# Attention operands staged by halves of the tokens, the first halves one head earlier

## The chip, the cores and the metric

The kernel runs on one core of a Trainium2 chip. Its engines are TensorE (PE in the profile, and PEld for its weight loads), VectorE (DVE), ScalarE (ACT), GpSimd (POOL) and SyncE (SP), which here only issues DMAs. They work side by side and wait for each other by semaphores. The metric is the device time of one execution in microseconds (us); less is better.

## The reference

The program is a two-layer encoder over 1024 tokens of width 1024, in float32. Layer 0 mixes tokens with a gated block, layer 1 with attention; each layer ends with a gated feed-forward with a short convolution. The change touches the attention of layer 1 alone:

```python
def chunk_attention(h, k, v, w_q, rel_bias, w_o):
    """Each 64-frame chunk attends to its own chunk and the previous 8 chunks."""
    q = (h @ w_q).reshape(B, nc, CHUNK, N_HEADS, HEAD_DIM) * scale
    ...
    bias = rel_bias[:, rel_idx]                       # 16 heads, clipped relative position
    sc = jnp.einsum('bqhd,bkhd->bhqk', qb, kb) + bias
    p = jax.nn.softmax(sc, axis=-1)
    o = jnp.einsum('bhqk,bkhd->bqhd', p, vb)
    return o @ w_o
```

There are 16 heads of width 64. A block of 128 queries sees its own block of keys and the four before it, so a block of 128 keys is seen by five blocks of queries.

## The kernel before, in words

Nearly all matrix products are done in three passes of a narrower format: each operand is split into a high part and a low rest, and the products high by high, low by high and high by low are summed. The attention runs over heads in pairs. The projections q, k and v of pair p+1 are computed 128 rows (two heads) at a time while pair p is attended to: six products (q, k, v, each for two halves of 512 tokens) of 24 matmuls, handed out by a generator called `fill`.

One head is eight steps, one per block of 128 keys. Step i of head hd does `head.score(i)` (matmuls "st", lines 1122 and 1124), some matmuls of `fill`, pieces of the next head's maximum (`Max.block`, matmuls "mx", lines 1076 and 1083), `value` of the block two steps back (matmuls "po", lines 1152 to 1156), and the rest of its share of `fill`. An even head (the first of a pair) gets 12 matmuls of `fill` in each step, an odd one 6. So an even head takes some 34 us and an odd one some 24 us.

A score product needs q and k of one head in four tiles of 128 partitions: KM and QE (high parts, with constant rows and a row for the maximum in the other 64 partitions), KS and QS (high and low parts mixed). There are two sets of them, for even and for odd heads. The function `stage` fills a set: one POOL memset of the maximum's row of QE (line 973) and six DMAs from the projection's tiles thi and tlo (line 976), issued by SP. In the kernel before, the six DMAs of head hd+1 are issued in step 0 of head hd, each over all 1024 tokens (64 partitions of 4 KB, 256 KB). Head 0 alone is staged by halves already.

`Max` of head hd+1 loads the head's bias table (line 1066) in step 1 of head hd and takes the maximum over blocks: block 0 at the end of step 1, block 1 in the middle of step 2, block 2 at its end, and so on; the blocks 0 to 3 read only the first 512 tokens of QE and KM. DVE reduces each (junk, ma and mb, lines 1079 and 1085). After block 7 the maximum is transposed ("mr", line 1092), copied by ACT (line 1095), and written by SP as one row of 4 KB into QE (line 1096). The next head's first score needs that row.

PE's order is the order of the program; the other engines' and SP's orders are chosen by a scheduler that simulates the program, and once chosen each queue is worked off in order, so a DMA on SP that waits for its data holds up all DMAs behind it.

Of the kernel before, what the change touches and what calls it, by code (L numbers as in the profile page):

```python
# [18 lines left out]
P = 128  # L19
T = 1024  # L20
# [7 lines left out]
NH = 16  # L28
# [13 lines left out]
def f32(ap):  # L42
    return ap.bitcast(F32)
# [3 lines left out]
def trunk(ctx: ExitStack, tc: tile.TileContext, x, a_win, a_wv, a_wst, a_bs, a_wout, w_kv, w_q, w_o,  # L47
          f_win, f_wdown, bias, cst, consts, fgain, out):
    nc = tc.nc
    V, S, G = nc.vector, nc.scalar, nc.gpsimd  # L50
# [15 lines left out]
    def put_off(us, fn):  # L66
        pending.append((clock[0] + us, len(pending), fn))
        pending.sort(key=lambda e: e[0])
# [12 lines left out]
    def open_psum(n, bufs, small=4):  # L81

        psum["ctx"], psum["n"] = ExitStack(), n
        psum["a"] = psum["ctx"].enter_context(tc.tile_pool(name="pj", bufs=bufs, space=PSUM, reuse_waits="tile"))
        open_small(small)

    def open_small(bufs=4):
        psum["s"] = psum["ctx"].enter_context(tc.tile_pool(name="sm", bufs=bufs, space=PSUM, reuse_waits="tile"))
# [21 lines left out]
    def close_psum():  # L110
        psum["ctx"].close()
# [40 lines left out]
    def load_w(src, gain=None, pool=None, new=None, lo=None):  # L152
        raw = new_raw([P, KD, P])
        nc.sync.dma_start(raw, src)
        if gain is not None:
            with tc.issue_after(behind[G].ins):
                G.tensor_tensor(raw, raw, cc[:, gain:gain + KD].unsqueeze(2).broadcast_to([P, KD, P]), op=ALU.mult)
        if pool:
            w = tuple(pool.tile([P, T], F32R, tag=n, name=n).rearrange("p (k c) -> p k c", c=P) for n in ("whi", "wlo"))
            split(*w, raw, lo or V)  # L160
            return w
        ws = [(new or new_w)() for _ in range(2)]
        for i in range(2):
            split(*ws[i], raw.rearrange("p k c -> p (k c)")[:, halves[i]], lo if lo and i else V)
        return tuple(Halves(t) for t in zip(*ws))
# [24 lines left out]
    halves = [slice(0, H), slice(H, T)]  # L190
# [739 lines left out]
    QE, QS, KM, KS = ([b0.tile([P, T], F32R, name=f"{n}0")] for n in ("qe", "qs", "km", "ks"))  # L930
# [33 lines left out]
            S.copy(vT, ps)  # L964
            put_off(1.2, lambda: transpose_v(vT, t, hi, lo))

    def stage(hd, cs=slice(0, T)):

        p, c = divmod(hd, 2)
        own, oth = rows[c]  # L970
        q, k = parts[p, "q"], parts[p, "k"]
        if cs.start == 0:
            G.memset(f32(QE[c][own.stop % P:own.stop % P + 1, :]), 0.0)
        for dst, src in ((KM[c][own], k[0]), (QE[c][own], q[0]), (QS[c][own], q[0]), (QS[c][oth], q[1]),
                         (KS[c][own], k[1]), (KS[c][oth], k[0])):
            nc.sync.dma_start(f32(dst[:, cs]), f32(src[own, cs]))
# [14 lines left out]
    first("q", 0)  # L991
    first("k", 0)
    stage(0, halves[0])
    proj(psv[:, H:T], w2["v"], ys[1])
    for what in "qk":
        ps2[what, 1] = psS("qk")
        proj(ps2[what, 1], w2[what], ys[1])
        first(what, 1)
    stage(0, halves[1])
    wv_ctx.close()  # L1000
    catch_up()
# [14 lines left out]
    def load_o(k, t):  # L1016
        os_[t][k] = oh, ol = new_y()
        nc.sync.dma_start(f32(oh), osave[0, k, :, halves[t]])
        behind["o"] = nc.sync.dma_start(f32(ol), osave[1, k, :, halves[t]])

    hr = []
    with tc.tile_pool(name="b1", bufs=1, reuse_waits="tile") as b1, \
# [33 lines left out]
        def stage_v(p):  # L1056
            for dst, src in zip((VH[1], VL[1]), parts[p, "v"]):
                nc.sync.dma_start(f32(dst[:, :, 64:P]), f32(src))
# [142 lines left out]
        catch_up()  # L1201
        close_psum()
        open_psum(H, 2)
        mx = Max(0)
        for b in range(NB):
            put_off(4.0 + 0.8 * b, lambda b=b: mx.block(b))
# [7 lines left out]
        def output(todo):  # L1214

            for m, load, bank in todo:
                w = load()
                ps = bank("wo")
                yield from products(ps, w, os_[0], range(LAST), None)
                outs.append((m, w, ps))  # L1220
# [6 lines left out]
        for s in range(NH * NB):  # L1227
            hd, i = divmod(s, NB)
            p, c = divmod(hd, 2)
            if i == 0:  # L1230
                if c == 0:
                    pair = Pair(p)
                head = Head(hd, mx.bt, pair.done)
                mx = None
            n = (6 if c else 12) + (1 - 2 * c if i == 0 else 0)
            if p == LAST - 1 and c:
                n = 6 if i < 4 else 3
            if p == 0:
                n = (144 - early) * (s + 1) // 16 - (144 - early) * s // 16
            if p == LAST:  # L1240
                n = 5
                if c == 0 and i == LAG + 1:
                    for k in range(LAST):
                        load_o(k, 0)
                    todo = [(m, lambda m=m: ws.pop(m), psP if m < 2 else psS) for m in range(6)]
                    fill = chain(fill, output(todo[:3]))
                if s - LAST * 2 * NB in loads:
                    m = loads.index(s - LAST * 2 * NB)
                    with ExitStack() as after:
                        for ins in marks:  # L1250
                            after.enter_context(tc.issue_after(ins.ins))
                        ws[m] = load_w(w_o[m]) if m < 2 else load_w(w_o[m], new=new_y, lo=G)
            if s == NH * NB - 6:

                for i2 in range(4):
                    place = f32(bt.tile([P, T], F32R, tag=("thi", "tlo")[i2 % 2], name="hr"))
                    for j in range(2):
                        hr.append(place[:, halves[j]])
                        with tc.issue_after(behind["o"].ins):
                            nc.sync.dma_start(hr[-1], hsave[1][2 * i2 + j, :, halves[0]])  # L1260
            head.score(i)
            waiting.append((head, i))
            if i == 0 and hd + 1 < NH:
                stage(hd + 1)
            if i == (LAG if p < LAST else 5) and c == 0:
                stage_v(p)
            for _ in range(n // 2):
                next(fill, None)
            if hd + 1 < NH:
                if i == 1:  # L1270
                    mx = Max(hd + 1)
                for b in mid.get(i, ()):
                    mx.block(b)
                if i == 6:
                    put_off(0.5, mx.row)
            if len(waiting) > LAG:
                h0, b = waiting.pop(0)
                h0.value(b)
            for _ in range(n - n // 2):
                next(fill, None)  # L1280
            if mx:
                for b in end.get(i, ()):
                    mx.block(b)
# [176 lines left out]
```

## Time and profile before

| | us |
|---|---|
| median of 3 runs | 2173.44 (2172.83 to 2175.77) |
| the profiled execution's own time | 2177.01 |
| its span, first to last instruction | 2175.2 |
| PE busy in the span | 2137.3 |
| DVE, ACT, POOL busy | 1589.7, 1088.0, 680.0 |
| mean granted TensorE clock | 0.995 of full speed |

The attention with its interleaved projections lies between about 980 and 1445 us of the span. A busy PE means that a matmul was in flight; where PE is idle, the timeline names in brackets the idle time and what ended it. A wait for several semaphores is put down to the one that came last by the profile, so the name in the bracket has to be held against the other candidates.

### The profile page before, as it was taken

Reading aid. Unit: us, or ns where it says so; the run is one execution under the profiler, and the core shown is the slowest. Engines: PE = TensorE matmul, PEld = TensorE weight load, DVE = VectorE, ACT = ScalarE, POOL = GpSimd, SP = SyncE. Lnnn points to the kernel's source line nnn. Section 1 sums busy time; section 2 is a strip of 40 time slices with the busy share of each in tenths; the row PEclk is TensorE's granted clock in tenths of the full one; section 3 lists DMA queues with packets and bytes.
Section 4 is the critical chain, followed back from the end, with each engine's and each line's share of the span. In section 5 each row is a group of like instructions: output and inputs, shape, how many; then the busy total and the mean of one; then the engine's idle time right before and its main releaser. Section 6 shows DMA issues by size and latency. Waiting matters only on the chain.

```text
span 2175.2 us, 28369 instructions
## 1 busy us (share of the span) xinstructions
PE 2137.3 (98%) x9940; PEld 1781.5 (82%) x9940; DVE 1589.7 (73%) x2425; ACT 1088.0 (50%) x1913; POOL 680.0 (31%) x472
## 2 busy tenths in 40 slices
PE   8999999999999999999999999899999999999998
PEld 6888887888888888878888888787878888888887
DVE  4762879888888757675676666764988888885676
ACT  6544445544455544445555555552554455554443
POOL 0301324242334212144444443351343333331020
PEclk9999999999999999999999999999999999999999
DMA  5242233344445867635444455644144444568553
GB/s 208 78 133 90 83 111 121 141 177 148 169 166 198 285 208 237 227 96 123 121 109 109 114 126 127 192 159 173 59 170 155 165 168 136 179 237 305 195 192 136
DMA packets 151536, 344.06 MB, mean 158 GB/s; under 512 B 31840, under 2 KB 32224, under 8 KB 151392
## 3 DMA queue, kind: packets, MB, share of 16 engines
q1 hardware_dynamic: 148368, 336.78, 47.7%
q10 hardware_dynamic: 3024, 5.46, 0.7%
q8 instruction: 78, 1.28, 0.2%
q14 instruction: 66, 0.54, 0.1%
HBM read 225.20 MB, written 87.56 MB: 144 GB/s over the span
## 4 chain that ended last, share of the span: by engine, by line
PE 85%; DVE 9%; ACT 2%; DMA 2%; issue 2%; POOL 0%; SPq 0%; DVEq 0%; POOLq 0%; ACTq 0%
PE gate L869 9%; PE up L869 9%; PE up L362 6%; PE up L364 6%; PE up L367 6%; PE gate L362 5%; PE gate L364 5%; PE gate L367 4%; PE vps L473 4%; PE qkv L186 4%; PE qkv L182 3%; PE qkv L179 3%; DVE wlo L138 2%; PE st L1122 1%; PE po L1156 1%
## 5 line engine op out<-in xcount | busy, mean ns | idle before, releaser
L138 DVE TENSOR_TENSOR wlo<-raw,whi 128x512 fp32r<-128x512 f32 (+1 forms) x424 | 374.0, 892 | 233.6 <-ACT whi L137 233.5
L137 ACT CAST whi<-raw 128x512 fp32r<-128x512 f32 (+1 forms) x428 | 266.5, 628 | 335.7 <-PE gate L869 201.9
L362 PE MATMUL up<-yh,whi 128*128 128x512 f32 x688 | 268.2, 390 | 0.8 <-ACT gate L765 0.5
L364 PE MATMUL up<-yh,wlo 128*128 128x512 f32 x688 | 267.9, 389 | 0.0
L1136 POOL TENSOR_TENSOR pl<-p,ph 128x640 fp32r<-128x640 f32 (+4 forms) x128 | 160.2, 1258 | 170.9 <-ACT ph L1135 112.9
L726 POOL TENSOR_TENSOR h<-a 128x512 f32<-128x512 f32 x44 | 77.9, 1771 | 391.4 <-DVE a L718 391.4
L362 PE MATMUL gate<-th,whi 128*128 128x512 f32 x496 | 193.4, 390 | 3.0 <-ACT h L703 1.8
L364 PE MATMUL gate<-th,wlo 128*128 128x512 f32 x496 | 193.0, 389 | 0.0
L367 PE MATMUL up<-yl,whi 128*128 128x512 f32 x688 | 183.9, 389 | 0.0
L362 PEld LDWEIGHTS up<-yh,whi 128*128 128x128 f32 x688 | 129.1, 188 | 29.3 <-ACT gate L765 2.7
L138 DVE TENSOR_TENSOR yl<-raw,yh 128x512 fp32r<-128x512 f32 x180 | 145.2, 811 | 10.6 <-ACT yh L137 10.4
L367 PEld LDWEIGHTS up<-yl,whi 128*128 128x128 f32 x688 | 129.1, 188 | 26.9
L364 PEld LDWEIGHTS up<-yh,wlo 128*128 128x128 f32 x688 | 129.1, 188 | 26.6
L182 PE MATMUL qkv<-yh,wlo 128*128 128x512 f32 x336 | 134.7, 401 | 0.0
L179 PE MATMUL qkv<-yh,whi 128*128 128x512 f32 x336 | 132.9, 395 | 0.0
L367 PE MATMUL gate<-tl,whi 128*128 128x512 f32 x496 | 132.6, 389 | 0.0
L137 ACT CAST whi<-S 128x512 fp32r<-128x512 f32 x160 | 99.1, 619 | 64.8 <-PE up L367 58.1
L869 PE MATMUL up<-yl,whi 128*128 128x512 f32 (+1 forms) x312 | 120.6, 387 | 0.0
L869 PE MATMUL up<-yh,whi 128*128 128x512 f32 (+1 forms) x312 | 120.4, 386 | 0.0
L869 PE MATMUL gate<-yh,wlo 128*128 128x512 f32 (+1 forms) x312 | 120.4, 386 | 0.0
L869 PE MATMUL up<-yh,wlo 128*128 128x512 f32 (+1 forms) x312 | 120.3, 386 | 0.0
L869 PE MATMUL gate<-yh,whi 128*128 128x512 f32 (+1 forms) x312 | 120.2, 385 | 0.0
(268 smaller groups left out, 5260.4 us busy)
## 6 DMA issues: line engine op xcount, KB each, us to landing
raw<-in_f_win SPq DMA_DIRECT2D x88, 512.0 KB
gT<-h SPq DMA_DIRECT2D x88, 256.0 KB
h<-in_f_wdown SPq DMA_DIRECT2D x44, 512.0 KB
dS<-h SPq DMA_DIRECT2D x88, 256.0 KB
raw<-dS SPq DMA_DIRECT2D x40, 512.0 KB
raw<-gT SPq DMA_DIRECT2D x40, 512.0 KB
gB<-a SPq DMA_DIRECT2D x66, 256.0 KB
raw<-in_f_wdown SPq DMA_DIRECT2D x30, 512.0 KB
```

What stands on the lines that cost most here:

```text
L137: behind[S] = S.copy(hi, src)
L138: return eng.tensor_tensor(lo, src, f32(hi), op=ALU.subtract)
L179: nc.tensor.matmul(ps, wh[:, k, :], xs[k][0], start=k == 0, stop=False)
L182: nc.tensor.matmul(ps, wl[:, k, :], xs[k][0], start=False, stop=False)
L186: nc.tensor.matmul(ps, wh[:, k, :], xs[k][1], start=False, stop=k == last)
L362: nc.tensor.matmul(ps, wh[:, k, :], xs[k][0], start=first and k == 0, stop=False, skip_group_check=True)
L364: nc.tensor.matmul(ps, wl[:, k, :], xs[k][0], start=False, stop=False, skip_group_check=True)
L367: nc.tensor.matmul(ps, wh[:, k, :], xs[k][1], start=False, stop=k == 3, skip_group_check=True)
L473: nc.tensor.matmul(ps, a, b, start=k == i == 0, stop=k == KD - 1 and i == 2)
L726: G.tensor_tensor(B[n], x, B.get(y) if isinstance(y, str) else y, op=ALU.subtract)
L869: nc.tensor.matmul(ps[:, cs], w[:, ms], x[:, cs], start=q == i == 0 and p in (1, 6, 5, 4), stop=q == NP - 1 and i == 2, skip_group_check=True)
L1136: marks[2] = G.tensor_tensor(pl[:, :n], pf[:, :n], f32(ph[:, :n]), op=ALU.subtract)
```

## The change

`stage` now always takes a half of the tokens. The second half of head hd+1 is staged where all of it was (step 0 of head hd); the first half of head hd+2 is staged in step 6 of head hd, the seventh step, so a step or two before head hd+1 begins and a full head before that head's own `Max` of hd+2 reads it. The set being filled is then the one that head hd itself is using; by step 6 only its second 512 tokens are still read. The first half of head 1, which has no head -1, is staged before head 0. The memset of QE's row goes by halves too. Each head so has 12 DMAs of 128 KB (64 partitions of 2 KB) where it had 6 of 256 KB, and two memsets of 512 elements for one of 1024.

```diff
-    def stage(hd, cs=slice(0, T)):
+    def stage(hd, cs):
...
-        if cs.start == 0:
-            G.memset(f32(QE[c][own.stop % P:own.stop % P + 1, :]), 0.0)
+        G.memset(f32(QE[c][own.stop % P:own.stop % P + 1, cs]), 0.0)
         for dst, src in ((KM[c][own], k[0]), (QE[c][own], q[0]), (QS[c][own], q[0]), (QS[c][oth], q[1]),
                          (KS[c][own], k[1]), (KS[c][oth], k[0])):
             nc.sync.dma_start(f32(dst[:, cs]), f32(src[own, cs]))
...
         open_psum(H, 2)
+        stage(1, halves[0])
         mx = Max(0)
...
             if i == 0 and hd + 1 < NH:
-                stage(hd + 1)
+                stage(hd + 1, halves[1])
+            if i == 6 and hd + 2 < NH:
+                stage(hd + 2, halves[0])
```

PE's order does not change at all. SP's changes as follows. The first place is the passage from head 2 (even) to head 3 (odd), as it repeats at every such passage: names ending in 8153 to 8156 are the even heads' set, 8463 to 8466 the odd heads'. Before:

```order
L154 DMA raw<-in_w_kv 128x1024
L1096 DMA qe_8463<-mr 1x8x128
L976 DMA qe_8153<-thi 64x1024
L976 DMA qs_8154<-thi 64x1024
L976 DMA qs_8154<-tlo 64x1024
L1066 DMA bias<-in_bias 128x512
L976 DMA km_8155<-thi 64x1024
L976 DMA ks_8156<-thi 64x1024
```

The same place on SP now (8464 is the odd heads' QE here):

```order
L975 DMA qe_8153<-thi 64x512
L975 DMA qs_8154<-thi 64x512
L975 DMA qs_8154<-tlo 64x512
L154 DMA raw<-in_w_kv 128x1024
L975 DMA km_8155<-thi 64x512
L975 DMA ks_8156<-thi 64x512
L975 DMA ks_8156<-tlo 64x512
L1095 DMA qe_8464<-mr 1x8x128
L975 DMA qe_8153<-thi 64x512
L975 DMA qs_8154<-thi 64x512
L975 DMA qs_8154<-tlo 64x512
L1065 DMA bias<-in_bias 128x512
```

Six half transfers now stand ahead of the row of the maximum, and six half transfers, not whole ones, behind it and around the bias.

The second place is SP at the passage from head 0 to head 1, where head 2 is staged. Before:

```order
L1096 DMA qe_8463<-mr 1x8x128
L976 DMA qe_8153<-thi 64x1024
L976 DMA qs_8154<-thi 64x1024
L976 DMA km_8155<-thi 64x1024
L976 DMA qs_8154<-tlo 64x1024
L976 DMA ks_8156<-tlo 64x1024
L976 DMA ks_8156<-thi 64x1024
L1066 DMA bias<-in_bias 128x512
```

Now:

```order
L1095 DMA qe_8464<-mr 1x8x128
L975 DMA qe_8153<-thi 64x512
L975 DMA qs_8154<-thi 64x512
L975 DMA km_8155<-thi 64x512
L975 DMA qs_8154<-tlo 64x512
L975 DMA ks_8156<-tlo 64x512
L975 DMA ks_8156<-thi 64x512
L1065 DMA bias<-in_bias 128x512
```

The bias stands behind half as many bytes; the other six halves stand ahead of the row of the maximum.

The third place is DVE at the start of head 14, where it works on the last projection's leftovers, on head 13's output and on head 15's maximum at once. Before:

```order
L1186 RECIPROCAL den<-den 128x128
L1128 TENSOR_TENSOR p<-st,bias 128x256
L1186 RECIPROCAL den<-den 128x128 x2
L1079 ISA junk,mb<-mx,bias 128x128
L1079 ISA mb 128x1
L138 TENSOR_TENSOR wlo<-raw,whi 128x512
```

Now:

```order
L1185 RECIPROCAL den<-den 128x128
L1078 ISA junk,mb<-mx,bias 128x128
L1078 ISA mb 128x1
L1127 TENSOR_TENSOR p<-st,bias 128x256
L1185 RECIPROCAL den<-den 128x128 x2
L138 TENSOR_TENSOR wlo<-raw,whi 128x512
```

The reduction of block 0 moved ahead of a score's bias addition and two reciprocals. In step 1 of head 1 the same reduction moved ahead of one bias addition. Apart from two pairs of neighbours on ACT and the memsets on POOL, nothing else moved.

## Rows read from the trace of the kernel before

**Rows 1.** The page: the span, and busy time by engine.
```profile
span 2175.2 us, 28369 instructions
...
PE 2137.3 (98%) x9940; PEld 1781.5 (82%) x9940; DVE 1589.7 (73%) x2425; ACT 1088.0 (50%) x1913; POOL 680.0 (31%) x472
```
**Rows 2.** PE's waits, 940 to 1445 us: total us, times, longest.
```profile
PE mx L1076 <- DVE o L1174: 5.8, 5, 1.5
PE st L1122 <- DVE mb L1079: 3.1, 2, 2.6
PE st L1122 <- DVE ma L1085: 2.2, 1, 2.2
PE st L1122 <- DMA qe<-mr: 1.8, 1, 1.8
...
PE mx L1076 <- DMA km<-thi: 1.1, 2, 0.9
```
**Rows 3.** Timeline of PE: start, us, instruction [idle before, what ended it].
```profile
1028.42 0.40 PE L1122 MATMUL st<-qe,km 128*128 128x256 f32 x1 [2.59 <-DVE mb L1079]
...
1084.09 0.30 PE L1076 MATMUL mx<-km,qe 128*128 128x128 f32 x1 [0.91 <-DMA km<-thi]
...
1142.56 0.30 PE L1076 MATMUL mx<-km,qe 128*128 128x128 f32 x1 [1.46 <-DVE o L1174]
...
1375.18 0.30 PE L1076 MATMUL mx<-km,qe 128*128 128x128 f32 x1 [0.62 <-DVE o L1174]
```
**Rows 4.** Timeline of SP (start, us to issue), odd heads 3, 5 and 13.
```profile
1074.21 0.72 SPq L1096 DMA_DIRECT2D qe<-mr  x1
...
1079.19 0.79 SPq L976 DMA_DIRECT2D km<-thi  x1
...
1137.12 0.81 SPq L976 DMA_DIRECT2D km<-thi  x1
...
1370.34 0.79 SPq L976 DMA_DIRECT2D km<-thi  x1
```
**Rows 5.** Timeline of DVE, the copy named in rows 2, heads 5 and 13.
```profile
1141.01 0.68 DVE L1174 COPY o<-po 64x512 f32<-64x512 f32 x1 [1.18 <-ACT den L1173]
...
1374.47 0.68 DVE L1174 COPY o<-po 64x512 f32<-64x512 f32 x1 [1.45 <-ACT den L1173]
```
**Rows 6.** Timeline of SP and of DVE in head 1.
```profile
1016.27 0.54 SPq L976 DMA_DIRECT2D qe<-thi  x1
...
1022.29 1.24 SPq L1066 DMA_DIRECT2D bias<-in_bias  x1
...
1028.07 0.29 DVE L1079 CUSTOM_DVE_ANT_0 junk<-mx,bias 128x128 f32<-128x128 f32 x1 [4.77 <-DMA bias<-in_bias]
```
**Rows 7.** Windows: us, busy us of five engines, granted clock, DMA share, GB/s.
```profile
1028.00:1032.00 4.00, 3.58 (x11) 3.11 (x12) 2.47 (x11) 1.62 (x3) 2.56 (x2) 0.58 0.02 7
...
1136.00:1140.00 4.00, 4.00 (x25) 3.51 (x23) 3.83 (x10) 3.62 (x8) 0.10 (x1) 1.00 1.00 229
...
956.00:962.00 6.00, 6.00 (x24) 4.51 (x23) 5.10 (x7) 2.86 (x5) 6.00 (x5) 0.92 0.61 143
```
**Rows 8.** Timeline, end of head 2: k's rest on DVE, head 3's first score.
```profile
1072.98 0.63 DVE L961 TENSOR_TENSOR tlo<-qkv,thi 128x512 fp32r<-128x512 f32 x1
...
1078.61 0.28 PE L1122 MATMUL st<-qe,km 128*128 128x256 f32 x1
```
**Rows 9.** Timeline, from head 1 to head 2: the maximum's row, the first score.
```profile
1042.04 0.70 SPq L1096 DMA_DIRECT2D qe<-mr  x1
...
1044.34 0.28 PE L1122 MATMUL st<-qe,km 128*128 128x256 f32 x1
```
**Rows 10.** Timeline of PE in head 14.
```profile
1406.19 0.58 PE L1122 MATMUL st<-qe,km 128*128 128x256 f32 x1 [2.22 <-DVE ma L1085]
...
1407.54 0.69 PE L1122 MATMUL st<-qe,km 128*128 128x384 f32 x1 [0.55 <-DVE mb L1079]
```
**Rows 11.** The memsets of line 973 on POOL: count, ns min/median/max, first and last.
```profile
L973 POOL MEMSET qe<- x16: 942/947/950, 940.1 to 1390.0; 1x1024 f32 x16
```

## The prediction

> **What bounds the kernel now.** I read the page first, then PE's waits in the attention, then the timelines around each wait. The page says that PE is busy for 2137.3 of 2175.2 us [rows 1]: whatever this change gives has to come out of the 38 us in which PE stands, and in the attention that is a handful of places. PE's waits from 940 to 1445 us name them [rows 2]. Two lines are about the matmul "mx": 5.8 us put down to a DVE copy (5 times) and 1.1 us put down to the DMA of km (twice). Three are about "st", and the longest of those is 2.6 us. The timeline shows where they stand. The mx waits are one per pair, always at the same matmul: block 0 of the next head's maximum, at the end of step 1 of an odd head [rows 3] (1084.09, 1142.56 and 1375.18 are three of six; the seventh of the two lines is 0.2 us in head 1). The 2.6 us are one wait in head 1, at 1028.42.
>
> What does the mx matmul really wait for? The label says a copy of o on DVE, and a label is only the last releaser that the profile knows. Between that copy's end and mx lie 0.87 us in head 5 (1141.69 to 1142.56) and 0.03 us in head 13 (1375.15 to 1375.18) [rows 3, 5]: no fixed distance, so it releases nothing. From the issue of km's DMA to mx it is 4.90, 5.44 and 4.84 us in heads 3, 5 and 13 [rows 3, 4]: a transfer's time, with the load of the queue in its scatter. So all six wait for km, whose transfer of all 1024 tokens can be issued only once the second half of k has been evacuated at the head's start. That is the first thing that the change removes.
>
> The wait in head 1 is of another kind. DVE's reduction of block 0 stood 4.77 us for the bias table [rows 6], the maximum's PSUM tiles stayed occupied, and PE ran out of them 2.59 us before 1028.42 [rows 3]. The bias was issued at 1022.29, behind six whole transfers whose first was issued at 1016.27 [rows 6], and landed about 1028.0.
>
> **Term 1: six waits for km, and 0.2 us in head 1.** Block 0 reads only the first 512 tokens. These are now issued a head ahead (in an odd head's queue the halves ahead of mr are the other set's), so when PE comes to mx they have been in place for some ten us. The second half is needed by block 4, two steps later, and is issued at the same time as before with half the bytes. In the instruction list of the changed kernel block 0 and block 4 each wait for DMAs of their own, so the parts are kept apart. Removed: 5.8 + 1.1 = 6.9 us [rows 2]. What is late next is DVE's reduction of block 0, which had been waiting for mx itself; PE has four tiles before it needs that one back.
>
> **Term 2: the bias in head 1.** From 1016.27 to 1028.0 the queue moved six times 0.262 MB and the bias' 0.262 MB, 1.83 MB in 11.8 us, or 156 GB/s. Now it is six times 0.131 and 0.262, 1.05 MB; at 156 GB/s that is 6.7 us, so the bias lands at about 1023.0. DVE began to wait at 1028.07 - 4.77 = 1023.3 [rows 6], PE at 1025.8. Removed: 2.59 us. After the wait the clock fell: in 1028 to 1032 the granted clock is 0.58 [rows 7], between 1.2 and 2.4 GHz, so 0.84 of 4 us ran at the lower level and half of it, 1.7 us, was lost. The short waits for km have no such window behind them. Removed with the wait: 1.7 us.
>
> **Term 3: DVE's order in head 14.** The reduction of block 0 moves ahead of an addition and two reciprocals, so the tile that 1407.54 waited for comes back earlier (0.55 us, [rows 10]), while the wait of 2.22 us before it, for a later reduction, stays. Between nothing and 2.77 us I take the nearer row, 0.5 us. The 1.8 us for the row of the maximum [rows 2] stay too, since there the row is late for want of matmuls to cover it.
>
> **What is added.** 90 DMA issues on SP (15 heads, 12 for 6) at 0.5 to 0.8 us each. SP stands idle for much of each head, so the issues cost nothing by themselves; what counts is what stands behind them. Ahead of mr there are now six halves. In an odd head their data has long been there and they are free once score 3 is issued, some ten us before mr. In an even head three of them wait for the first half of k: the last for its rest, which DVE ends at 1072.98 + 0.63 = 1073.61 [rows 8]. Its issue takes about 0.6 us, so mr, issued at 1074.21 before [rows 4], goes out 0.1 to 0.6 us later, and its 4 KB run behind 0.13 to 0.4 MB. At the 229 GB/s of a full DMA window [rows 7] that is 0.6 to 1.7 us. Head 3's first score starts 4.40 us after mr's issue [rows 4, 8], and where an odd head ends 2.30 us are enough with no wait of PE [rows 9]. The slack is 2.1 us, the delay 0.7 to 2.3: hidden but for perhaps 0.2 us in some heads. I charge 0.3 us in all. The bounds: no cost, and 1.3 us a passage if all six were ahead (0.79 MB at 229 GB/s are 3.4 us, less 2.1).
>
> Do halves cost more per byte? The trace has six: those of head 0 from 956.5 on. In 956 to 962 the DMA engines moved 143 GB/s at a share of 0.61 [rows 7], 234 GB/s for a full share, against 229 for whole ones. So no.
>
> The Trainium skill, "DMA: Bandwidth & Descriptors", section "Anatomy of one DMA", speaks against the change: it puts a fixed 2 us on each DMA, whatever its size (measured there on GpSimd's path). If those added up, six halves in a row would be late by nearly as much as six wholes, and term 2 would be gone. The window of head 0's halves does not bear it out: they overlap.
>
> The memsets become two of 512 elements for one of 1024 at 0.95 us [rows 11]: the same elements, between 0 and 0.95 us more per head on POOL. The first waits in POOL's queue for score 3 just ahead of the subtraction that needs score 3 itself, so it holds up nothing that could have run. No cost.
>
> **Sum**: 6.9 + 2.6 + 1.7 + 0.5 - 0.3 = 11.4 us. The profiled execution took 2177.0 us, so 2165.6; it was 3.6 us above the median of the three runs, and against that median of 2173.4 the forecast is 2162 us, 0.5% faster.
>
> **Rivals.**
> *The label is right (12%).* If mx does wait for DVE's copy, the 5.8 us of the five waits stay [rows 2], and the gain is 5.6: 2168 us. For it: five of seven waits carry that name. Against it: the uneven distances above.
>
> *Halves take as long as wholes (12%).* Then the bias lands as late as before and term 2 stays: gain 11.4 - 4.3 = 7.1, 2166 us. For it: descriptors of half the size, twice as many. Against it: the window at 956.
>
> *Both, or the km wait gives way to another one (8%).* A gain of 0 to 4 us, no change that can be told: 2171 us. PE has no other wait in those steps now, but nothing shows how near the next one is.
>
> *Slower: the row of the maximum lands behind the halves (7%).* Place: mr at every passage. If all six halves are still in flight when it is issued, it lands 3.4 us later. At the seven passages into an odd head 2.1 of these are hidden, 1.3 are not; at the seven into an even head, whose 2.30 us leave next to nothing [rows 9], 3.4 cost in full: 7 x 4.7 = 33 us, 2195 us. It decides from a mean of 1.1 us lost per passage on, where the 14 passages take up the 11.7 us gained and 4.3 more. For it: three of the halves in an even head are issued within two us of mr. Against it: in odd heads, where the slack is small, they are ten us ahead.
> The Trainium skill ("DMA: Bandwidth & Descriptors", "Queues, rings and completion order") says that what one engine issues goes through one ring on each DMA engine and is worked off in ring order. By that rule the row cannot pass the halves; no row here shows the two next to each other.
>
> **Numbers.** The forecast has 61%, with a range of its own from 2157 to 2166. The range for eight in ten takes in the two rivals beside it and the bounds of terms 2 and 3: 2157 to 2170. About 0.2%, 4.3 us, is what a measurement of this kernel can tell from no change. Faster: 61 + 12 + 12 = 85%; the same 8%; slower 7%.
>
> **What would show it.** In the new profile PE's waits for mx at the end of step 1 of odd heads are gone (right) or stand there with the same 0.6 to 1.5 us (the label was right). The bias of head 1's reduction lands before 1024 us and the granted clock near 1030 is 1.00. The issue of mr to the next first score is still 4.4 us in even and 2.3 us in odd heads, without a wait. New waits of PE for "qe<-mr" would make the prediction wrong on the slower side; new waits for DVE's reductions in place of km would make it wrong on the side of no change.

## The result, and the profile after

The changed kernel takes 2161.1 us (median of 4 runs, 2159.2 to 2164.8) beside 2174.6 us for the kernel before (4 runs, 2172.8 to 2176.7). The ratio is 0.9935, with a 95% interval from 0.9922 to 0.9947. The forecast was 2162 us, 0.5% faster; it is 0.65% faster by this ratio, 0.62% by the medians. The profiled execution took 2162.3 us.

Line numbers from `stage` on are one lower than before (mx 1075, st 1121, mr 1091, the scaling on POOL still 157). The page of the new profile, its span and busy times, answers to [rows 1]:

```profile
span 2160.5 us, 28590 instructions
...
PE 2131.3 (99%) x9940; PEld 1777.6 (82%) x9940; DVE 1592.7 (74%) x2425; ACT 1087.9 (50%) x1913; POOL 680.6 (31%) x488
```

PE's idle time went from 37.9 to 29.2 us, and its busy time fell by 6.0 us with the same 9940 matmuls, for the most part because less of it lies at the lower clock (below). PE's waits in the attention, the largest of 935 to 1445 us (total, times, longest), answer to [rows 2]:

```profile
PE st L1121 <- DVE mb L1078: 3.1, 1, 3.1
...
PE mr L1091 <- DVE mb L1086: 1.4, 1, 1.4
...
PE st L1121 <- DMA qe<-mr: 1.2, 1, 1.2
```

No line with mx and km or with the copy of o is left, and the 3.1 us are another wait than before: it stands in head 14, not in head 1. From 994.7 to 1380 us, so from head 0 to the end of head 13, no wait of PE is left. The timeline of PE at the end of step 1 of head 3, where [rows 3] had 0.91 us, now reads:

```profile
1078.62 0.40 PE L182 MATMUL qkv<-yh,wlo 128*128 128x512 f32 x1
1078.86 0.23 PE L1075 MATMUL mx<-km,qe 128*128 128x128 f32 x1
1078.91 0.33 PE L1121 MATMUL st<-qe,km 128*128 128x256 f32 x1
```

The mx matmul starts without a bracket, 0.24 us behind its predecessor's start, and takes 0.23 us where after a wait it took 0.30. In head 1, the bias on SP, DVE's first reduction and the window that [rows 6, 7] showed:

```profile
1021.03 0.59 SPq L1065 DMA_DIRECT2D bias<-in_bias  x1
```
```profile
1024.19 0.29 DVE L1078 CUSTOM_DVE_ANT_0 junk<-mx,bias 128x128 f32<-128x128 f32 x1 [0.41 <-DMA bias<-in_bias]
```
```profile
1028.00:1032.00 4.00, 4.00 (x27) 3.64 (x26) 2.54 (x11) 2.54 (x6) 2.95 (x3) 1.00 0.78 182
```

DVE waits 0.41 us for the bias where it waited 4.77, PE not at all, and the granted clock is 1.00 (of 2.4 GHz) where it was 0.58. The bias is issued in 0.59 us, where it took 1.24 behind six whole transfers.

Where the time went, head by head: I take the start of the first "st" matmul behind each "mr" matmul as a mark (for head 0 its first score, from then on the score of the eighth step of the head in front), and the gain of a head is its distance between two marks before less the same distance in another kernel (us; "start" is the mark of head 0, before less that kernel).

| kernel | start | head 1 | 3 | 5 | 7 | 9 | 11 |
|---|---|---|---|---|---|---|---|
| the change | -1.11 | 5.00 | 1.17 | 1.70 | 1.71 | 1.15 | 1.63 |
| split_only | -0.41 | 5.00 | 1.17 | 1.70 | 1.70 | 1.16 | 1.63 |
| bias_first | 1.34 | 2.56 | 0.37 | 0.59 | 0.71 | -0.04 | 1.41 |
| km_split | -0.05 | 0.91 | -0.11 | 0.49 | 0.60 | -0.17 | 1.63 |
| late_bias_first | -8.85 | 5.00 | 1.16 | 1.71 | 1.70 | 1.15 | 1.64 |
| km_split_pool | 1.52 | 1.10 | 1.17 | 1.70 | 1.71 | 1.15 | 1.63 |
| km_pool_bias | 2.36 | 5.00 | 1.16 | 1.70 | 1.71 | 1.15 | 1.63 |

For the change, heads 13 and 14 add 2.7 us together, and the even heads 4 to 12 lie within 0.01 us of before. The column "start" also holds the 980 us ahead of the attention, where PE does the same work in all these kernels and yet the executions lay apart: at the matmul that starts at 975 us in the kernel before, km_pool_bias was 2.25 us ahead of it, km_split_pool 1.42, bias_first 1.21, split_only 0.57, the change 0.31, and km_split and late_bias_first 0.17 and 0.31 behind. Without that, the start itself costs the change 1.4 us, split_only 1.0 and late_bias_first 8.5; the other four gain 0.1. The table's other kernels are the experiments, which follow.

### The profile page after: what moved, and what is told of

Its sections match the earlier page's. It is cut to its first block, busy times and chain, and to the rows that moved or that the text cites. A ratio compares the mean times of both kernels' runs of the same rounds, so it can differ in the third digit from the quotient of the medians.

```text
span 2160.5 us, 28590 instructions
## 1 busy us (share of the span) xinstructions
PE 2131.3 (99%) x9940; PEld 1777.6 (82%) x9940; DVE 1592.7 (74%) x2425; ACT 1087.9 (50%) x1913; POOL 680.6 (31%) x488
## 4 chain that ended last, share of the span: by engine, by line
PE 85%; DVE 9%; DMA 2%; ACT 2%; issue 1%; POOL 0%; DVEq 0%; SPq 0%; POOLq 0%; ACTq 0%
PE gate L869 9%; PE up L869 9%; PE up L362 6%; PE up L364 6%; PE up L367 6%; PE gate L362 5%; PE gate L364 5%; PE gate L367 5%; PE vps L473 4%; PE qkv L182 4%; PE qkv L179 4%; PE qkv L186 3%; DVE wlo L138 2%; PE po L1155 1%; PE po L1153 1%
```

## The experiments

**split_only: the place of the calls.**
```diff
-        stage(1, halves[0])
...
             if i == 0 and hd + 1 < NH:
-                stage(hd + 1, halves[1])
-            if i == 6 and hd + 2 < NH:
-                stage(hd + 2, halves[0])
+                for hs in halves:
+                    stage(hd + 1, hs)
```


> The changed kernel, but both halves of a head's transfers are called for in step 0 of the head in front; the calls in the seventh step, and the one ahead of head 0's maxima, are gone. What stays of the change is the split alone. Theory A (the split makes the whole gain; the place of the call decides nothing, since every transfer goes as soon as its source is written and its buffer free): the same time as the changed kernel, 2161 us within 2, ratio to the kernel before 0.993 to 0.994, and the same waits of PE. Theory B (the early call carries the gain): the first halves are issued later, waits for km of 0.5 to 1.5 us come back in the odd heads, and the time lies at 2166 to 2172 us.

Measured: 2164.5 us, ratio 0.9945 (0.9928 to 0.9962), and the gain of the heads 1 to 13 is the change's. The instruction lists of the two kernels are the same on all engines, so theory A holds, though the time lies 1.5 us above its range: the seventh step decides nothing, and what differs between the two is what one list does from execution to execution. In these two traces that is 0.4 us at the start and 0.7 us in the wait for the row of the maximum at head 14 (1.16 us in the change, 1.90 here); the medians lie 3.4 us apart, the ratios 0.0010. The scheduler issues a transfer as soon as its source is written and its buffer free, and a half is ready earlier than a whole.

**bias_first: the bias ahead of the wholes.**
```diff
             if i == 0 and hd + 1 < NH:
+                mx = Max(hd + 1)
                 stage(hd + 1)
...
-                if i == 1:
-                    mx = Max(hd + 1)
```


> The kernel before with one edit: the bias of the next head's maxima is called for ahead of the six whole transfers in step 0, so that SP issues it ahead of them. Theory A (the terms are separate: in head 1 the bias came late because six whole transfers stood in front of it, in the odd heads km came late because its own transfer is long): the 2.59 us wait in head 1 and the stretch at clock 0.58 go, 4.3 to 5.0 us; the waits for km in the odd heads stay, each 0 to 0.6 us longer since one more transfer is ahead of km. Time 2167 to 2172 us, ratio 0.9965 to 0.9990. Theory B (both waits come from the traffic of the whole transfers, and only halves take them away): the bias still lands late in head 1, and the time stays at 2173 to 2175 us.

Measured: 2168.6 us, ratio 0.9962 (0.9947 to 0.9976). The time is theory A's, the reason is neither's: the km waits went in all odd heads from 3 on but head 7 (0.74 us there), and head 1 gained half of what it should. SP's timeline of this kernel at the passage to head 3, to be held against [rows 4]:

```profile
1071.72 0.53 SPq L976 DMA_DIRECT2D qe<-thi  x1
1072.35 0.53 SPq L1066 DMA_DIRECT2D bias<-in_bias  x1
...
1075.58 0.46 SPq L976 DMA_DIRECT2D km<-thi  x1
```

From the first transfer's issue to km's are 3.86 us in both kernels, and the same four transfers stand ahead of km. But with the bias second, 189 GB/s were moved in the 4 us from the first issue, before 145; km then was there for an mx that ran 7.7 us after that issue, where before it was not at 7.8 us. Why the order of the four changes the rate is left open. PE waited elsewhere instead, here in head 1:

```profile
1031.43 0.39 PE L1156 MATMUL po<-pl,vh 128*128 128x256 f32 x1 [1.67 <-POOL pl L1136]
```

**km_split: one transfer of the six by halves.**
```diff
+        for part in (halves if cs == slice(0, T) else (cs,)):
+            nc.sync.dma_start(f32(KM[c][own, part]), f32(k[0][own, part]))
-        for dst, src in ((KM[c][own], k[0]), (QE[c][own], q[0]), ...
+        for dst, src in ((QE[c][own], q[0]), ...
```


> The kernel before with one edit: of a head's six transfers only km's is split by halves, the other five stay whole. Theory A (the first block of maxima waits for the length of km's one transfer, and half of it is enough): the six waits for km at the odd heads go, 6.9 us by PE's idle and up to 8.2 us by the starts of the heads; the bias in head 1, behind seven transfers now, is as late as before, so that its 2.59 us wait and its slow clock stay. Time 2166 to 2169 us, ratio 0.9960 to 0.9975. Theory B (the wait named km was the traffic of all six, or DVE's copies that feed the transfers): waits of 1 us or more stay at the odd heads, 2172 to 2175 us.

Measured: 2167.2 us, ratio 0.9957 (0.9943 to 0.9972). PE waits for km at no odd head any more, as theory A has it. In head 5, where the label put the wait down to DVE's copy of o, mx now starts before that copy does, so the copy cannot be what it waits for. PE and then DVE, to be held against [rows 3, 5]:

```profile
1140.12 0.23 PE L1078 MATMUL mx<-km,qe 128*128 128x128 f32 x1
```
```profile
1140.19 0.68 DVE L1176 COPY o<-po 64x512 f32<-64x512 f32 x1 [1.17 <-ACT den L1175]
```

But heads 3 to 9 give back nearly all of it at once. POOL's timeline at head 3, and then PE's:

```profile
1083.29 1.58 POOL L1138 TENSOR_TENSOR pl<-p,ph 128x640 fp32r<-128x640 f32 x1 [0.82 <-ACT ph L1137]
1088.35 1.90 POOL L157 TENSOR_TENSOR raw<-raw,cc 128x1024 f32<-128x1024 f32 x1 [3.48 <-DMA raw<-in_w_q]
1090.21 3.06 POOL L1138 TENSOR_TENSOR pl<-p,ph 128x640 fp32r<-128x640 f32 x2
```
```profile
1091.81 0.39 PE L1158 MATMUL po<-pl,vh 128*128 128x256 f32 x1 [1.03 <-POOL pl L1138]
```

The scaling of the next pair's q weights (L157) stands in POOL's queue ahead of the third pl and waits 3.48 us for its own transfer, and PE then waits for pl. The same row was there before, and the wait for km had covered it:

```profile
1088.88 1.90 POOL L157 TENSOR_TENSOR raw<-raw,cc 128x1024 f32<-128x1024 f32 x1 [3.11 <-DMA raw<-in_w_q]
```

SP issues that transfer last, and this is where the change differs (km_split first, then the change):

```profile
1080.38 0.69 SPq L978 DMA_DIRECT2D ks<-tlo  x1
1081.16 2.17 SPq L154 DMA_DIRECT2D raw<-in_w_q  x1
```
```profile
1076.97 0.46 SPq L975 DMA_DIRECT2D ks<-tlo  x1
1077.53 0.54 SPq L154 DMA_DIRECT2D raw<-in_w_q  x1
```
```profile
1081.90 1.90 POOL L157 TENSOR_TENSOR raw<-raw,cc 128x1024 f32<-128x1024 f32 x1 [0.27 <-DMA raw<-in_w_q]
```

With halves the issue takes 0.54 us, not 2.17, and POOL (last fence) waits 0.27 us: it starts on the weights 11.0 us behind head 3's mark, 14.2 in km_split and 13.8 before. Heads 11 and 13 scale no q weights any more, and there km_split has the whole gain: 1.63 us in head 11.

**late_bias_first: halves, held behind the row of the maximum.**
```diff
+                behind["mr"] = nc.sync.dma_start(f32(QE[self.c][row:row + 1, :]), f32(mr))
...
-        stage(1, halves[0])
...
             if i == 0 and hd + 1 < NH:
+                mx = Max(hd + 1)
+                with tc.issue_after(behind["mr"].ins):
+                    stage(hd + 1, halves[0])
                 stage(hd + 1, halves[1])
-            if i == 6 and hd + 2 < NH:
-                stage(hd + 2, halves[0])
```


> The changed kernel with the early part undone by force: the halves are called for in step 0, the first halves are held until SP has issued the row of the maximum, and the bias is called for ahead of them. Order on SP at a passage: mr, km's first half, bias, the other first halves, the second halves. Theory A (short transfers and a bias in front of them are enough, being early is not needed): no km wait, no bias wait, the time of the changed kernel within 3 us, 2158 to 2164. Theory B (the first halves must be under way ahead of the row of the maximum): waits of 1 to 1.5 us at the odd heads come back, some of the even heads wait too, and the time lies at 2167 us or above.

Measured: 2168.8 us, ratio 0.9968 (0.9957 to 0.9978). The total is theory B's, the heads are theory A's: from head 1 on each gains what it does in the change (head 6 lies 0.1 us under it). The loss is one wait of PE ahead of head 0's first score, with the clock at 0.50 from 1000.2 to 1006.8 behind it, and ACT's row says for whom:

```profile
1001.34 0.80 PE L179 MATMUL qkv<-yh,whi 128*128 128x512 f32 x1 [5.51 <-DVE tlo L958]
```
```profile
999.97 1.08 ACT L957 ACTIVATE thi<-qkv 128x512 fp32r<-128x512 f32 x2 [3.42 <-DMA qs<-thi]
```

The held halves of head 1 are still to be read from the tiles that the next projection writes. So early transfers are not needed for their own readers, with the bias in front as here; at the start they free their source. POOL has the scaling behind the third pl here, by the scheduler's own choice, and although the weights are issued only at 1088.46, behind twelve halves, PE does not wait for pl.

**km_split_pool: that instruction on POOL moved one place.** To km_split is added:
```diff
-            with tc.issue_after(behind[G].ins):
+            with tc.issue_after((behind.get("pl", behind[G]) if gain == C_BG else behind[G]).ins):
...
             head.score(i)
+            if c and i == 2 and p < LAST:
+                behind["pl"] = marks[2]
```


> The kernel before with km's transfer alone split by halves, as in the run of that edit, and one instruction moved besides: on POOL the scaling of the next pair's q weights (raw by cc) is held behind the third score's subtraction (pl) of an odd head, where it stood behind the second. Theory A (once km is early, PE's next wait in the odd heads, 1.03, 0.94, 0.83 and 1.06 us for pl in heads 3, 5, 7 and 9, is the weights' transfer: it lands late behind the whole transfers and the scaling that waits for it holds up pl in POOL's queue): these four waits go, 3.9 to 4.8 us, and the time lies at 2162 to 2164 us, ratio 0.9935 to 0.9950; head 1 still waits for its bias. Theory B (pl is late for another reason, POOL's own work or the memset of 1024 elements): the waits stay, 2166 to 2168 us.

Measured: 2165.8 us, ratio 0.9950 (0.9937 to 0.9962), a little above theory A's time. The four waits for pl are gone and heads 3 to 9 gain exactly what they do in the change. POOL at head 3 now reads, and the scaling's transfer is as late as ever (2.02 us to issue, at 1079.06):

```profile
1081.43 3.24 POOL L1138 TENSOR_TENSOR pl<-p,ph 128x640 fp32r<-128x640 f32 x2 [0.82 <-ACT ph L1137]
1086.13 1.90 POOL L157 TENSOR_TENSOR raw<-raw,cc 128x1024 f32<-128x1024 f32 x1 [1.46 <-DVE ma L1087]
```

**km_pool_bias: and the bias first.** To this is added the edit of bias_first.

> The kernel of the run above (km alone split, the scaling on POOL one place later) with the bias of the next head called for ahead of the other transfers as well. Theory A (three things make up the change's gain: km early, the bias not behind six whole transfers, the weights' scaling not in front of pl): head 1 gains 4.1 us more, by its 2.1 us wait and the slow clock behind it, and the time is that of the changed kernel or a little under, 2157 to 2161 us, ratio 0.9915 to 0.9935, with 15 more transfers than before where the change has 90 more. Theory B (the bias in front delays km's halves or the row of the maximum in other heads): waits for km or for the row come back, 2163 us or above.

Measured: 2161.5 us, ratio 0.9929 (0.9916 to 0.9943), theory A's ratio and half a us above its time. Head 1 has its 5.00 us, and no wait for km or a new one for the row came. So km early, the bias not behind six wholes and the weights not in front of pl make up the change's gain in the heads 1 to 11, with 15 more transfers where the change has 90. The two cannot be told apart in time.

**tail: head 14.** To the change:
```diff
-    ... else (2.0, 0.5))[t] + (1.2 if t else 2.0) * i, ...
+    ... else (2.0, 8.0))[t] + (1.2 if t else 2.0) * i, ...
```


> The changed kernel with one number changed: the pieces of head 13's second half of output, normalised on DVE at the start of head 14, are due 7.5 us later. Theory A (the 3.15 us wait of PE in head 14 is the reduction of a maximum that stands on DVE behind this output's reciprocals and products): the wait shrinks by 1.5 to 3 us and the time with it, 2158 to 2160 us, ratio 0.9915 to 0.9930. Theory B (the reduction waits for something else, or the output comes late for the projection behind it): no gain, 2161 us or above.

Measured: 2160.0 us, ratio 0.9927 (0.9914 to 0.9939). The largest wait of the change, and the window around it in the change and in tail:

```profile
1391.79 0.58 PE L1121 MATMUL st<-qe,km 128*128 128x256 f32 x1 [3.15 <-DVE mb L1078]
```
```profile
1390.00:1395.00 5.00, 3.21 (x10) 2.61 (x11) 5.00 (x14) 1.64 (x4) 0.64 (x1) 0.50 0.49 164
```
```profile
1390.00:1395.00 5.00, 5.00 (x30) 4.55 (x29) 4.13 (x16) 2.16 (x5) 2.66 (x3) 1.00 0.87 282
```

The wait and the low clock are gone. In their place PE waits in tail at the end of the head:

```profile
1401.07 0.27 PE L1091 MATMUL mr<-ident,mb 128*8 128x128 f32 x1 [2.10 <-DVE mb L1086]
...
1404.76 0.38 PE L1121 MATMUL st<-qe,km 128*128 128x256 f32 x1 [0.83 <-DMA qe<-mr]
```

From head 14's first score (1380.07 in the change, 1379.70 here) to head 15's (1407.93, 1404.76) are 27.9 us in the change and 25.1 here, 2.8 us less, as theory A has it. PE's idle time between these marks fell only from 4.6 to 3.9 us; the other 2 us are the clock, which was at 0.50 from 1389.1 to 1395.9 in the change, with PE busy for some 4 of these 6.8 us, and is 1.00 throughout here (an estimate: half of 4). The runs' intervals overlap with the change's.

**best and later.** best is km_pool_bias with tail's edit; later has 14.0 in place of 8.0.

> The three edits to the kernel before (km alone split, the bias called for first, the weights' scaling behind the third pl) together with the later due time of head 13's second half of output (8.0 for 0.5). Theory A (the two gains lie at different places, 5 us in head 1 and 8 in the odd heads on one side and 3 to 4 us in head 14 on the other, and so add): 2156 to 2159 us, ratio 0.9900 to 0.9920, and no wait of PE of 3 us left in head 14. Theory B (head 14's gain was the changed kernel's own order on DVE): the wait in head 14 stays and the time is that without the edit, 2160 to 2162 us.

> As the run beside it, with the output due at 14.0 for 8.0: its last reciprocals and products then stand behind the reduction that gives head 15's row of the maximum, where at 8.0 PE still waited 2.10 us for that reduction and 0.83 us for the row. Theory A (these 2.9 us are DVE's queue): they shrink by 1.5 to 2.9 us, 2153 to 2157 us. Theory B (the row is late for want of matmuls of PE in head 14, or the output is then late for the projection that reads it): no further gain, within 1 us of the run beside it or slower.

Measured: best 2158.6 us, ratio 0.9927 (0.9913 to 0.9940); later 2164.8 us, 0.9948 (0.9936 to 0.9961). In best, at theory A's time and a ratio just above its range, the wait of 3 us is gone and head 14 is as short as in tail. In the traces the two gains add as theory A has it: between 975 and 1440 us best gains 17.7 us on the kernel before, km_pool_bias 15.4. The ratios are the same within their intervals, so the sum is not shown in the time. Behind the attention best gives back 1.3 us against km_pool_bias, most of it a wait of 1.18 us for DVE's addition in the output projection. The change has such a wait too (1.2 us) and split_only, with the same list, has none, so it is no price of the edit. In later the reduction is in time, but the row is not, and the copy of head 14's output stands behind the moved pieces:

```profile
1403.79 0.39 PE L1124 MATMUL st<-qe,km 128*128 128x256 f32 x1 [3.97 <-DMA qe<-mr]
...
1414.75 0.33 PE L1154 MATMUL po<-ph,vh 128*128 128x128 f32 x1 [3.21 <-DVE o L1176]
```

So theory B: best's two waits there, 2.10 and 0.87 us, became one of 3.97. No version here beats the changed kernel by more than the measurement can tell; best and tail have the lowest medians.

## Why the prediction was right, and where it was not

- *What the mx matmul waits for.* Right: km, not the copy that the label names. In km_split only km is earlier, and mx of head 5 starts 0.07 us before the copy.
- *Term 1, 6.9 us.* The heads 3 to 11 gained 7.36 us. Their waits were 0.91, 1.46, 1.47, 0.90 and 1.39, 6.13 us: each wait cost 0.24 to 0.26 us more than its idle time. Some 0.16 us of it is the overlap of neighbouring matmuls (those of 0.40 us start 0.24 apart) and 0.07 the first matmul after the wait, 0.30 for 0.23.
- *"What is late next is DVE's reduction of block 0".* This step failed, and the sum hid it. Next was POOL's scaling, which waits for the weights behind the six transfers. Had the change only brought km forward, as in km_split, heads 3 to 9 would have given 0.8 us in all instead of 5.7. The change pays because the same halves let the weights land earlier too. The prediction did not know of that, so in these four heads its number is right by luck.
- *Term 2, 4.3 us, and 0.2 for head 1's small wait.* Right in kind, head 1 gained 5.00. The bias was there at about 1024.2, not 1023.0 and just past the 1024 named as the sign (the whole timeline is 1.0 us late there), soon enough. Its price was also POOL's: with the bias early and the wholes left, 1.67 us came back for pl.
- *Term 3, 0.5 us.* 1.16 us, from head 14's first score to head 15's (29.02 to 27.86), but not for the reason given. The 0.55 us wait went and one of 1.47 became 0.67, while the 2.22 us became 3.15 and a new one of 0.64 came: PE's idle time between these marks is 4.5 us before and 4.6 in the change. What fell is the time at the lower clock, from two stretches to one; the windows inside them, two before and one in the change:

```profile
1394.00:1397.20 3.20, 3.20 (x11) 2.71 (x11) 1.30 (x3) 1.61 (x3) 1.41 (x1) 0.50 0.96 201
1404.20:1410.90 6.70, 4.15 (x13) 3.65 (x14) 6.69 (x19) 2.77 (x6) 1.83 (x2) 0.50 0.55 192
```
```profile
1389.20:1395.80 6.60, 4.01 (x13) 3.41 (x14) 6.60 (x19) 1.97 (x5) 1.87 (x2) 0.50 0.54 171
```

PE was busy for all of the first, so half of its 3.2 us, 1.6 us, is an estimate of what its going gave. DVE's order changed more than the part ahead of the prediction lists: in the traces the three reductions behind the one named moved forward in head 14 as well. Why the first stretch is gone is not shown; split_only, with a longer wait for the row just ahead, has none either.
- *The row of the maximum, 0.3 us.* At the end of head 2 ACT had copied it at 1070.0 and SP issued it at 1070.51, 0.5 us late, within the 0.1 to 0.6 expected, and PE waited for it at no passage but the one into head 14, where it did so before (1.82 us, then 1.16; 1.90 in split_only, so the 0.66 us gained there are not the change's). Head 3's first score came 3.9 us behind the row's issue, without a wait, where it came 4.4 behind it before. The even heads lost nothing; the rival on the slower side did not occur.
- *"Issued a head ahead".* The prediction gave this the credit. split_only shows that the seventh step does not matter, late_bias_first that the readers do not need the early issue (there the bias was called for first as well).
- *Not foreseen: the start*, 1.4 us lost (below).

Between the medians lie 13.5 us for the 11.4 of the sum, between the two profiled spans 14.7; from 975 us to the end of the attention the traces have 13.9. To the 11.4 come what the waits cost beyond their idle time (1.2 us in heads 3 to 11, 0.3 in head 13, 0.5 in head 1), 0.7 in term 3, 0.7 in the wait for the row into head 14, the 0.3 charged for the row and 0.3 in heads 0 and 2; the start takes 1.4 off. So the total came nearer to the forecast than its parts because the loss at the start offset some of the rest.

## What to carry to other kernels

When a wait is removed, look on every queue for who is idle beside it: POOL's 3.11 us in front of L157 were in the old trace, hidden by 0.91 us of km. Splitting transfers pays here by what stands behind them on the queue (the bias, the weights), and where a scheduler places DMAs the line where one is called for may decide nothing. Calling the load that is read first ahead of the others, splitting the one transfer that PE waits for and moving one instruction did as much as splitting all six. And two executions of one instruction list lay 0.7 us apart in a single wait: a gain of that size is not read from one trace.

## What the runs showed of the hardware that was not expected

At the start DVE's last step before the row of the maximum (128x6, usually 0.22 us) took 1.83 us in the change, beside POOL's scaling. DVE's row and POOL's:

```profile
992.82 1.83 DVE L1086 SCALAR_TENSOR_TENSOR mb<-ma,cc,mb 128x6 f32<-128x6 f32 x1
```
```profile
992.73 1.90 POOL L157 TENSOR_TENSOR raw<-raw,cc 128x1024 f32<-128x1024 f32 x1 [4.87 <-DMA raw<-in_w_kv]
```

Both end within 0.02 us of each other, at 994.65 and 994.63, and PE waits 1.37 us. It is so in split_only (993.97 and 993.95) and tail (994.31 and 994.30) too. In km_split (DVE at 993.30, POOL from 995.44) and km_split_pool (991.73, 994.32) the two do not meet, and DVE takes 0.23 us. The same step of DVE stands at the end of every head. In the eleven traces it starts 58 times while this scaling runs and ends 0.02 to 0.03 us behind it every time, after 0.25 to 1.83 us; in 11 more it does so behind a pl; in the 104 with nothing running on POOL it takes 0.22 or 0.23 us. So in every case seen this step of DVE lasts until the instruction of POOL that began before it has ended. No run was made for this alone, and which operands make them meet is open. The change brings these weights to POOL earlier, into that meeting, and the start is 1.4 us longer; in the kernels where the two do not meet it is not.

The issue of a DMA on SP mostly takes 0.3 to 0.8 us, but often 1.2 to 2.2 us behind several whole transfers (the bias 1.24 before and 0.59 after, the weights 2.17 in km_split and 0.54 in the change): SP itself is held up, and all that stands behind it. Between 980 and 1445 us, 63 issues of the kernel before take over 1 us, and 8 of the change, with more DMAs. In km_pool_bias 37 do, and heads 1 to 11 gain the same, so their number alone does not decide.
